# A 64-byte offset between TensorE's loaded and streamed operands in a one-core hybrid decoder trunk

## The chip, the cores and the metric

The kernel runs on one core of a Trainium2 chip. The metric is the device time of one execution in microseconds (us). TensorE multiplies, VectorE, ScalarE and GpSimd (POOL in the profile) do the elementwise work, and the queue of SyncE (SP) issues the DMAs. The other cores are idle.

## The reference

A trunk of two residual layers works on one sequence of 2048 tokens of width 1024, in float32. Each layer is `x = x + rms_norm(layer(rms_norm(x, g)), g2)`.

```python
# layer 0: one input projection, then two groups of heads
parts = jnp.split(h @ w_in, _offsets(EVEN_SPLIT_SIZES), axis=-1)
q, kc, vc, ks, vs, kw, vw, g_logit, z_a, u, v, z_b = parts
a = nsa_attention(q, kc, vc, ks, vs, kw, vw, g_logit, ...) * jax.nn.silu(z_a)
b = spatial_gating(jax.nn.gelu(u), jax.nn.gelu(v), ...) * jax.nn.silu(z_b)
return jnp.concatenate([a, b], axis=-1) @ w_out
# layer 1: a convolution module
a, gl, z = jnp.split(h @ w_in, 3, axis=-1)
y = a * jax.nn.sigmoid(gl)
y = depthwise_causal_conv(y, dw_w, 31 taps) + dw_b
y = jax.nn.silu(layer_norm(y, ln_g, ln_b))
return (y * jax.nn.silu(z)) @ w_out
```

`nsa_attention` has 8 heads of 64 in 2 groups, and adds three branches by gates: over 127 compressed blocks, over the 8 blocks of 64 tokens that score best for a query, and over a window of 512 tokens.

## The kernel before

Nearly every product is made of three matmuls. A float32 operand is split into a high part in the format float32r and a low part, the rest (`split`, L112 to L119), and `hi*hi + hi*lo + lo*hi` is summed in PSUM. A matmul names two operands: the first is loaded into the array as weights, 128 columns at a time, the second streams past it, 128 to 512 columns long. In the profile's rows the streamed one stands first (`A<-hhi,whi` streams `hhi` past `whi`). Each matmul has a weight load of its own, and the load for the next matmul runs while the present one streams.

- `project` (twice, for 1024 tokens each) makes the input projections. `dense_T` (L155 to L157) loads weights and streams 512 tokens of the normalised input; `dense_N` (L167 to L171) loads 128 tokens and streams 256 or 280 weight columns. `load_w` fetches and splits a block of weights. The spatial mix (L355) loads `sw`.
- `attention` walks over 64 units of a query tile, a head group and a pair of heads. `scores` (L570, L571) loads `q` and streams K, in pieces of 128 to 512 columns. The probabilities are transposed (L702: the probabilities are loaded, the identity of 128 columns streams), split, and streamed past V, 256 columns at a time (L724, L725). The front part of a unit (scores and softmax) is interleaved with the back part of the unit before. q is loaded by DMA four units ahead, V and K when a query tile first needs them.
- `out1` and `out2` (`out_project`, L836 to L838) load 128 tokens (`b4`, or the tiles `h2`, `h3`, `h6`, `h7`) and stream 512 columns of the output weights. A quarter of the first output weights is kept in the buffers of V's last two chunks.
- `layer1_in` makes layer 1's projections with `dense_T`, 24 blocks of 256 weight columns, each with four groups of 24 matmuls. Beside it VectorE and GpSimd run the convolution, by a written table of beats of 5.12 us: VectorE a tap at L1128, ScalarE and GpSimd another at L1094 and L1095.

The order of the instructions is set when the program is built, by a scheduler over the emitted work. `tile` takes every buffer from a pool. `LINE = 256`: tiles of under 1024 bytes a partition that aren't a multiple of 256 bytes go to a pool of their own, and two unused tiles at the edges (`LEFT`, `RIGHT`) bring all pools to multiples of 256 bytes. So in the built program the loaded and the streamed operand both start at a multiple of 256 bytes in all but three of 12388 matmuls (those three lie 128 off, both of them alike).

Of the kernel before, what the change touches and what calls it, by code (L numbers as in the profile page):

```python
# [11 lines left out]
F32R = mybir.dt.float32r  # L12
# [7 lines left out]
P = 128  # L20
S = 2048
D = 1024
KT = D // P
# [14 lines left out]
FILL = 8  # L38
EARLY = 20
LINE = 256  # L40
LEFT, RIGHT = 96, 224
LATE = 2
OUT1 = [5, 7, 6, 4, 1, 3, 2, 0, *range(8, NT)]
# [37 lines left out]
class Trunk:  # L81
# [18 lines left out]
        self.keep.append(p)  # L100
        return p

    def tile(self, pool, shape, dt, tag, bufs=None):

        kw = {} if bufs is None else {"bufs": bufs}
        title, space, usual = self.pools[id(pool)]
        size = (2 if dt == BF16 else 4) * math.prod(shape[1:])
        if space is None and size % LINE and size < 1024:
            pool, tag, kw = self.odd, f"{title}_{tag}", {"bufs": bufs or usual}
        return pool.tile(shape, dt, name=self.name(tag), tag=tag, **kw)  # L110
# [16 lines left out]
        g.memset(e, -0.5)  # L127
        g.tensor_tensor(out, x, e, ALU.pow)

    def load_w(self, pool, pieces, home=None, hi_eng=None):  # L130

        nc = self.nc
        n = sum(p.shape[1] for p in pieces)
        room = -(-n // 64) * 64
        raw = self.tile(pool, [P, KT, room], F32, "wraw", 1)[:, :, :n]
        o = 0
        for p in pieces:
            w = p.shape[1]
            nc.sync.dma_start(raw[:, :, o:o + w], p.rearrange("(k p) n -> p k n", p=P))
            o += w  # L140
        where, tags = (self.rp, home) if home else (pool, ("whi", "wlo"))
        hi, lo = (self.tile(where, [P, KT, room], F32R, t)[:, :, :n] for t in tags)
        self.split(hi, lo, raw, hi_eng or nc.scalar, nc.vector if home else nc.gpsimd)
        return hi, lo

# [109 lines left out]
    def setup_sgu(self, pool):  # L255
        nc, a = self.nc, self.a
        wn = self.tile(pool, [P, D], F32, "xin", 4).rearrange("p (g j) -> p g j", g=8)
        nc.sync.dma_start(wn, a["even_sgu_w"][0].rearrange("g i j -> i g j"))
        nc.gpsimd.affine_select(out=wn, in_=wn, pattern=[[0, 8], [-1, P]], compare_op=ALU.is_ge,
                                fill=0.0, base=0, channel_multiplier=1)  # L260
        sw = self.tile(pool, [P, 2, 8, P], F32R, "sw")
        self.sw_hi, self.sw_lo = sw[:, 0], sw[:, 1]
        for q in range(2):
            pt = self.tile(self.ps, [P, 512], F32, "T", 3)
            for g in range(4):
                nc.tensor.transpose(pt[:, P * g:P * g + P], wn[:, 4 * q + g], self.ident)
            v = lambda t: t[:, 4 * q:4 * q + 4].rearrange("p g i -> p (g i)")
            self.split(v(self.sw_hi), v(self.sw_lo), pt, nc.scalar, nc.vector)
        self.sb = self.tile(pool, [P, 8], F32, "sb")
        nc.sync.dma_start(self.sb, a["even_sgu_b"][0].rearrange("g i -> i g"))  # L270
        self.sg = self.tile(pool, [P, 2, 512], F32, "sg")
        nc.sync.dma_start(self.sg[:, 0], a["even_sgu_ln_g"][0:1, :].to_broadcast([P, 512]))
        nc.sync.dma_start(self.sg[:, 1], a["even_sgu_ln_b"][0:1, :].to_broadcast([P, 512]))


    def project(self, half):
        nc, a = self.nc, self.a
# [3 lines left out]
        col = lambda c0, n: W[:, c0:c0 + n]  # L281
# [11 lines left out]
            h0 = next(self.first)  # L293
        else:
            h0 = self.h0
        wv = [self.load_w(self.wp, [col(C_V, 256)], hi_eng=nc.vector if half == 0 else None)]
        x1 = self.load_rows(self.rp, rows(t0 + 512), ("r2", "r3"))
        for _ in self.first:
            pass
# [19 lines left out]
                nc.sync.dma_start(dst[1, f:f + P, s], lo.bitcast(F32))  # L319

        gvs = [self.tile(self.rp, [P, 4, 512], F32, f"r{c}") for c in range(2)]
        wv.append(self.load_w(self.wp, [col(C_V + 256, 256)], hi_eng=nc.gpsimd))
        for i, w in enumerate(wv):
            for t in range(8):
                o = self.tile(self.ps, [P, 512], F32, "A")
# [56 lines left out]
        for i in range(2):  # L382
            w = self.load_w(self.wp, [col(C_Q + 256 * i, 256)])
            for j in range(2):
                f = 256 * i + P * j
# [161 lines left out]
    def load_q(self, qt, g):  # L547

        nc, ap = self.nc, self.ap_
        q = self.tile(ap, [P, 2, 4, P], F32R, "q", 4)  # L550
        src = self.q_d[:, 256 * g:256 * g + 256, P * qt:P * qt + P].rearrange("y (h d) t -> y d h t", d=64)
        for y, x in itertools.product(range(2), range(2)):
            nc.sync.dma_start(q[64 * x:64 * x + 64, y].bitcast(F32), src[y])
        return q
# [188 lines left out]
    def fill(self):  # L743

        for _ in self.rest:
            pass
        self.psx.close()
        self.pst = self.pool(self.psx, "pst", 1, PSUM)
        self.rx.close()
        self.w1x = self.ctx.enter_context(ExitStack())  # L750
        self.w1p = self.pool(self.w1x, "w1", side="right")
        self.kv2 = self.pool(self.w1x, "kv2", side="right")
        for c in (2, 3):
            self.V[c] = self.tile(self.kv2, [P, 4, 4, P], F32R, f"V{c}")

    def attention(self):
        units = [(qt, g, p) for qt in ATTENTION for g in range(2) for p in range(2)]
# [142 lines left out]
    def out1(self, banks):  # L900

        nc, a, lp = self.nc, self.a, self.lp
        order = OUT1
        slots = ("wraw", "whiA", "wloA")
        raws = dict(enumerate(self.raws))

        def load(n):
            if n < NT:
                raws[n] = self.tile(lp, [P, 16, P], F32, slots[(n + 2) % 3])
                self.load_raw(raws[n], order[n])  # L910

        w = self.w1
        places = [None, None, None, [(self.kv2, "Ps", 2)] * 2]
        for store in self.stores:
            store()
        gpost = self.load_gpost(0)
        last = lambda: self.wout_pieces(a["even_w_out"][0], [(lp, f"h{i}") for i in range(4, 8)], places, (3,), w, nc.gpsimd)
        hs, xs = {}, []
        for n, i in enumerate(order):
            s = P * i  # L920
            load(n + 2)
            raw = raws.pop(n)
            if n > 1:
                nc.scalar.activation(raw[:, 12:16], raw[:, 12:16], AF.Silu)
                nc.gpsimd.tensor_tensor(raw[:, 4:8], raw[:, 4:8], raw[:, 0:4], ALU.add)
                nc.vector.tensor_tensor(raw[:, 4:8], raw[:, 4:8], raw[:, 12:16], ALU.mult)
            lhs = [self.tile(lp, [P, KT, P], F32R, "b4", 5) for _ in range(2)]
            self.split(*lhs, raw[:, 4:12], nc.scalar, nc.vector)
            done = n in (4, 8)
            if done:  # L930
                first, norm, xs = min(i for i, _ in xs), [x for _, x in sorted(xs, key=lambda e: e[0])], []
            out = self.out_project(lhs, w, gpost, a["x"][0, s:s + P, :], self.x1_d[s:s + P, :], banks=banks)
            if n == 0:
                next(out)
                held = out, i
                continue
            if n == 1:
                last()
            if n == 1:
                next(out)  # L940
                *_, x = held[0]
                xs.append((held[1], x))
            *_, x = out
            xs.append((i, x))
            if done:
                hs[first // 4] = self.normed(lp, norm, self.gpre[:, 1], self.chunk_tags(first // 4),
                                             lambda k: self.tile(banks[k % 2], [P, 512], F32, "T", 1))
        return [hs[0], hs[1]]


    def layer1_in(self, inner, half, hs):
# [5 lines left out]
        def load():  # L957
# [12 lines left out]
                nc.sync.dma_start(raw[:, :, o:o + w], p.rearrange("(k p) n -> p k n", p=P))  # L970
                o += w
            where, tag = ((pool, "A"), (inner, "B"))[i % 2]
            hi = self.tile(where, [P, KT, 256], F32R, "whi" + tag)
            lo = self.tile(where, [P, KT, 256], F32R, "wlo" + tag)
            self.split(hi, lo, raw, nc.scalar, nc.gpsimd)
            self.busy("p", 4.5)
            self.ws.append((hi, lo))
# [191 lines left out]
    def gated_norm(self, c, hand):  # L1169
# [77 lines left out]
            nc.gpsimd.tensor_tensor(y, y, z, ALU.mult)  # L1247
        self.busy("p", 4.5)
        yield
        hi, lo = (self.tile(pool, [P, KT, 256], F32R, f"h{2 + 4 * (c % 2) + i}") for i in range(2))  # L1250
        for q, y in enumerate(Y):
            s = slice(4 * q, 4 * q + 4)
            self.split(hi[:, s], lo[:, s], y, nc.scalar, nc.gpsimd)
# [90 lines left out]
    def run(self):  # L1344
# [1 line left out]
        mid = self.ctx.enter_context(ExitStack())  # L1346
        c = self.pool(mid, "mid")
        self.Kc = self.tile(c, [P, 2, P], F32R, "Kc")
        self.Vc = self.tile(c, [P, 2, P], F32R, "Vc")
        self.gates = self.tile(c, [P, NT, 24], F32, "gates")  # L1350
        self.rx = self.ctx.enter_context(ExitStack())
        self.rp = self.pool(self.rx, "right", side="right")
# [7 lines left out]
        with ExitStack() as ctx:  # L1360
            self.kvx = ctx
            kv = self.pool(ctx, "kv")
            self.V = {c: self.tile(kv, [P, 4, 4, P], F32R, f"V{c}") for c in (1, 0)}
            self.K = self.tile(kv, [P, 2, 2, S], F32R, "K")
            self.ps = self.pool(ctx, "psa", 3, PSUM)
            self.psx = ctx.enter_context(ExitStack())
            self.psf = self.pool(self.psx, "psf", 1, PSUM)
            self.pst = None
            self.probs = self.pool(ctx, "probs")
            self.ap_ = self.pool(ctx, "attn")  # L1370
            self.attention_consts(self.ap_)
            self.attention()
# [32 lines left out]
```

## Time and profile before

| | |
|---|---|
| median of 3 runs | 2283.37 us (2282.74 to 2284.02) |
| the profiled execution | 2281.41 us |
| its span on the core | 2279.7 us |
| granted clock of TensorE, mean | 0.993 |
| TensorE busy, matmuls | 2206.6 us (97%), 12414 instructions |
| weight loads busy | 1911.1 us (84%), 12414 |
| VectorE busy | 1548.0 us (68%) |
| ScalarE busy | 1258.4 us (55%) |
| GpSimd busy | 1403.2 us (62%) |

Busy times are unions of the spans of an engine's instructions. Spans of matmuls overlap, as one still drains when the next begins, so neither the mean of one nor the busy share tells how fast they follow each other; that is read from their starts in the timeline. PE is TensorE's matmuls, PEld its weight loads.

### The profile page before, as it was taken

The numbers are of one execution on the slowest core, as the hardware profiler recorded it, in microseconds if no ns is written. First come the engines' busy times: TensorE is split into PE (matmuls) and PEld (weight loads), VectorE is DVE, ScalarE is ACT, GpSimd is POOL, SyncE is SP. The second block draws the span as 40 slices with busy tenths as digits, with TensorE's granted clock in tenths as the row PEclk, the third lists the DMA queues.
The fourth block names the chain that finished last, engine by engine and source line by source line (L and its number), as shares of the span: only waits on it lengthen the run. The fifth ranks groups of instructions, "written<-read, shape, count | busy, mean of one in ns | idle before, by whom it ended". The sixth has DMA issues, their size and how long they took to land.

```text
span 2279.7 us, 34587 instructions
## 1 busy us (share of the span) xinstructions
PE 2206.6 (97%) x12414; PEld 1911.1 (84%) x12414; DVE 1548.0 (68%) x3272; ACT 1258.4 (55%) x2345; POOL 1403.2 (62%) x1351
## 2 busy tenths in 40 slices
PE   8999999999989999999999989999999989998998
PEld 7898889988878999898998978888888778886877
DVE  3441324365248998888889944427998899999772
ACT  5241132253257888878888863426555575556463
POOL 5232222243237778667779645558999579999683
PEclk9999999999999999999999999999999999999999
DMA  6252231442381111101113144651222432224641
GB/s 159 95 188 90 79 107 53 141 139 78 91 239 52 36 41 29 29 20 27 29 54 110 43 158 152 217 196 47 83 74 84 139 111 65 74 93 146 224 166 65
DMA packets 244860, 229.19 MB, mean 101 GB/s; under 512 B 33841, under 2 KB 206897, under 8 KB 244432
## 3 DMA queue, kind: packets, MB, share of 16 engines
q1 hardware_dynamic: 244688, 226.98, 31.4%
q8 instruction: 98, 1.61, 0.3%
q14 instruction: 74, 0.61, 0.1%
HBM read 157.73 MB, written 69.21 MB: 100 GB/s over the span
## 4 chain that ended last, share of the span: by engine, by line
PE 66%; DVE 12%; POOL 10%; issue 5%; ACT 4%; DMA 2%; SPq 1%; DVEq 0%; POOLq 0%; ACTq 0%
POOL cacc L1095 8%; PE A L155 7%; PE A L156 7%; PE A L157 7%; PE T L702 7%; PE O L725 4%; PE A L570 4%; PE O L724 4%; DVE acc L1128 4%; PE A L836 4%; PE A L837 4%; PE A L838 4%; PE A L571 4%; PE A L169 2%; PE A L171 2%
## 5 line engine op out<-in xcount | busy, mean ns | idle before, releaser
L1128 DVE SCALAR_TENSOR_TENSOR acc<-y,const_taps,acc 128x1024 f32<-128x1024 f32 x304 | 378.9, 1281 | 4.0
L1095 POOL TENSOR_TENSOR cacc<-cacc,prod 128x1024 f32<-128x1024 f32 x145 | 371.4, 2567 | 15.0 <-ACT prod L1094 7.7
L119 POOL TENSOR_TENSOR wlo<-wraw,whi 128x2048 fp32r<-128x2048 f32 (+1 forms) x26 | 120.7, 4642 | 315.1 <-ACT whi L116 279.9
L119 DVE TENSOR_TENSOR ptl<-T,pth 128x512 fp32r<-128x512 f32 (+1 forms) x414 | 263.7, 659 | 20.5 <-ACT pth L116 17.8
L116 ACT CAST pth<-T 128x512 fp32r<-128x512 f32 (+1 forms) x414 | 221.6, 579 | 52.5 <-PE T L702 42.1
L1094 ACT ACTIVATE prod<-y,const_taps 128x1024 f32<-128x1024 f32 x145 | 165.2, 1149 | 140.7 <-POOL cacc L1095 140.5
L155 PE MATMUL A<-hhi,whi 128*128 128x512 f32 x608 | 238.3, 392 | 0.0
L157 PE MATMUL A<-hhi,wlo 128*128 128x512 f32 x608 | 237.4, 391 | 0.0
L156 PE MATMUL A<-hlo,whi 128*128 128x512 f32 x608 | 237.4, 390 | 0.0
L679 POOL TENSOR_SCALAR Ps<-Ps,attn_ssm,gates 128x256 f32<-128x256 f32 (+15 forms) x128 | 162.0, 1266 | 112.7 <-DVE attn_ssm L676 78.5
L725 PE MATMUL O<-ptl,V 128*128 128x256 f32 x824 | 221.9, 295 | 1.6 <-DVE ptl L119 0.6
L724 PE MATMUL O<-pth,V 128*128 128x256 f32 x824 | 223.2, 293 | 0.0
L570 PE MATMUL A<-K,q 128*128 128x320 f32 (+4 forms) x544 | 206.8, 384 | 7.8 <-DVE attn_smx L574 4.5
L571 PE MATMUL A<-K,q 128*128 128x320 f32 (+4 forms) x544 | 183.5, 343 | 0.0
L674 ACT ACTIVATE Ps<-Ps,attn_nm 128x256 f32<-128x256 f32 (+15 forms) x128 | 155.8, 1217 | 31.9 <-DVE attn_nm L672 29.9
L574 DVE CUSTOM_DVE_ANT_1 Ps<-A,attn_bm 128x512 f32<-128x512 f32 (+3 forms) x264 | 154.9, 611 | 24.3 <-PE A L571 12.5
L702 PE MATMUL T<-ident,Ps 128*128 128x128 f32 x1088 | 164.2, 273 | 2.4 <-DVE ptl L119 1.6
L725 PEld LDWEIGHTS O<-ptl,V 128*128 128x128 f32 x824 | 155.9, 189 | 9.2 <-DVE ptl L119 4.7
L724 PEld LDWEIGHTS O<-pth,V 128*128 128x128 f32 x824 | 156.1, 189 | 2.5
L155 PE MATMUL A<-h,whiB 128*128 128x512 f32 x384 | 149.6, 390 | 1.3 <-ACT b L1019 1.3
L156 PE MATMUL A<-h,whiA 128*128 128x512 f32 x384 | 150.8, 393 | 0.0
L155 PE MATMUL A<-h,whiA 128*128 128x512 f32 x384 | 149.8, 392 | 0.7 <-DVE y L1001 0.7
(388 smaller groups left out, 6203.6 us busy)
## 6 DMA issues: line engine op xcount, KB each, us to landing
wraw<-in_even_w_in_dram SPq DMA_DIRECT2D x24, 1024.0 KB, 6.0
q<-q_d SPq DMA_DIRECT2D x128, 128.0 KB, 2.9
wraw<-in_odd_w_in_dram SPq DMA_DIRECT2D x32, 512.0 KB, 4.6
x<-x_d SPq DMA_DIRECT2D x21, 512.0 KB, 3.4
a_d<-osum SPq DMA_DIRECT2D x128, 64.0 KB, 2.1
x<-in_x_dram SPq DMA_DIRECT2D x16, 512.0 KB, 5.5
x_d<-x SPq DMA_DIRECT2D x16, 512.0 KB, 2.6
wraw<-in_odd_w_in_dram SPq DMA_DIRECT2D x8, 1024.0 KB, 4.9
```

Source lines behind the costliest of these rows:

```text
L116: self.nc.scalar.copy(hi, src)
L119: lo_eng.tensor_tensor(lo, src, hi.bitcast(F32), ALU.subtract)
L155: nc.tensor.matmul(o, whi[:, k, wk], hhi[:, k], start=(k == 0), stop=False)
L156: nc.tensor.matmul(o, whi[:, k, wk], hlo[:, k], start=False, stop=False)
L157: nc.tensor.matmul(o, wlo[:, k, wk], hhi[:, k], start=False, stop=(k == KT - 1))
L570: nc.tensor.matmul(out, q[:, 0, r, :], K[:, g, ks], start=True, stop=False)
L571: nc.tensor.matmul(out, q[:, 1, r, :], K[:, g, ks], start=False, stop=True)
L702: nc.tensor.transpose(pt[:, c:c + P], ps[r], self.ident)
L724: nc.tensor.matmul(O, v, hi[:, c], start=(i + j == 0), stop=False)
L725: nc.tensor.matmul(O, v, lo[:, c], start=False, stop=(i + j == len(items) - 1))
L1095: nc.gpsimd.tensor_tensor(c["sum"], c["sum"], t, ALU.add)
L1128: v.scalar_tensor_tensor(acc, win, w, old, ALU.mult, ALU.add)
```

## The change

`tile` gets a parameter `shift`. With it, the tile is allocated 64 elements (256 bytes) longer, and the slice that begins `shift` elements in is used; an element has 4 bytes, so 16 are 64 bytes and 48 are 192. The shift is given to the tiles that matmuls load: the split weights of `load_w` (by default 16), the spatial mix's `sw`, `q`, V, the left halves of the output projections (`b4`, `h2`, `h3`, `h6`, `h7`), layer 1's weights and `Vc`. The blocks `wv`, which stream in `dense_N`, get 48, so that the unshifted loaded halves of the input lie 64 bytes ahead of them.

```diff
+OFF = 16
...
-    def tile(self, pool, shape, dt, tag, bufs=None):
+    def tile(self, pool, shape, dt, tag, bufs=None, shift=0):
+        if shift:
+            n = math.prod(shape[1:])
+            t = self.tile(pool, [P, n + LINE // 4], dt, tag, bufs)[:, shift:shift + n]
+            a = "abc"[:len(shape) - 1]
+            return t.rearrange(f"p ({' '.join(a)}) -> p {' '.join(a)}", **dict(zip(a, shape[1:])))
...
-    def load_w(self, pool, pieces, home=None, hi_eng=None):
+    def load_w(self, pool, pieces, home=None, hi_eng=None, shift=16):
...
-        hi, lo = (self.tile(where, [P, KT, room], F32R, t)[:, :, :n] for t in tags)
+        hi, lo = (self.tile(where, [P, KT, room], F32R, t, shift=shift)[:, :, :n] for t in tags)
...
-        sw = self.tile(pool, [P, 2, 8, P], F32R, "sw")
+        sw = self.tile(pool, [P, 2, 8, P], F32R, "sw", shift=OFF)
...
-        wv = [self.load_w(self.wp, [col(C_V, 256)], hi_eng=nc.vector if half == 0 else None)]
+        wv = [self.load_w(self.wp, [col(C_V, 256)], shift=3 * OFF, hi_eng=nc.vector if half == 0 else None)]
...
-        wv.append(self.load_w(self.wp, [col(C_V + 256, 256)], hi_eng=nc.gpsimd))
+        wv.append(self.load_w(self.wp, [col(C_V + 256, 256)], shift=3 * OFF, hi_eng=nc.gpsimd))
...
-        q = self.tile(ap, [P, 2, 4, P], F32R, "q", 4)
+        q = self.tile(ap, [P, 2, 4, P], F32R, "q", 4, shift=OFF)
...
-            self.V[c] = self.tile(self.kv2, [P, 4, 4, P], F32R, f"V{c}")
+            self.V[c] = self.tile(self.kv2, [P, 4, 4, P], F32R, f"V{c}", shift=OFF)
...
-            lhs = [self.tile(lp, [P, KT, P], F32R, "b4", 5) for _ in range(2)]
+            lhs = [self.tile(lp, [P, KT, P], F32R, "b4", 5, shift=OFF) for _ in range(2)]
...
-            hi = self.tile(where, [P, KT, 256], F32R, "whi" + tag)
-            lo = self.tile(where, [P, KT, 256], F32R, "wlo" + tag)
+            hi = self.tile(where, [P, KT, 256], F32R, "whi" + tag, shift=OFF)
+            lo = self.tile(where, [P, KT, 256], F32R, "wlo" + tag, shift=OFF)
...
-        hi, lo = (self.tile(pool, [P, KT, 256], F32R, f"h{2 + 4 * (c % 2) + i}") for i in range(2))
+        hi, lo = (self.tile(pool, [P, KT, 256], F32R, f"h{2 + 4 * (c % 2) + i}", shift=OFF) for i in range(2))
...
-        self.Vc = self.tile(c, [P, 2, P], F32R, "Vc")
+        self.Vc = self.tile(c, [P, 2, P], F32R, "Vc", shift=OFF)
...
-            self.V = {c: self.tile(kv, [P, 4, 4, P], F32R, f"V{c}") for c in (1, 0)}
+            self.V = {c: self.tile(kv, [P, 4, 4, P], F32R, f"V{c}", shift=OFF) for c in (1, 0)}
```

On every engine the built program has the same instructions in the same order as before. Six of them differ in the semaphores that they wait for: four on GpSimd in the first output projection, one on SyncE there, and one on VectorE at the start of attention. The addresses in the built program stand like this, modulo 256 bytes:

| matmuls | loaded minus streamed, before | after | streamed at, after |
|---|---|---|---|
| 512 columns, 6032 | 0 | 64 | 0 |
| 512 columns on V's buffers, 192 | 0 | 0 | 64 |
| 384 and 320 columns, 464 | 0 | 64 | 0 |
| 280 columns, 384 | 0 | 192 | 64 |
| 256 columns, 1952 | 0 | 64 | 0 |
| 256 columns of `wv`, 768 | 0 | 64 | 192 |
| 128 columns of the scores, 336 | 0 | 64 | 0 |
| transposes, 2106 | 0 | 0 | 0 |
| others, 154 | 0 | 0 | 0 or 128 |

## Rows read from the trace of the kernel before

**Rows 1.** The page of the profiled execution, its first line.

```profile
span 2279.7 us, 34587 instructions
```

**Rows 2.** Busy time by stage, all engines: stretch, length, busy and (instructions) of each.

```profile
core 0: us, PE busy (x) PEld busy (x) DVE busy (x) ACT busy (x) POOL busy (x), PEclk, DMA share, GB/s
0.00:640.00 640.00, 623.61 (x3461) 545.53 (x3462) 240.79 (x360) 201.61 (x347) 181.74 (x139) 0.99 0.37 113
640.00:1330.00 690.00, 671.11 (x4929) 617.26 (x4927) 589.07 (x2274) 570.28 (x1342) 504.43 (x869) 1.00 0.20 56
1330.00:1540.00 210.00, 203.80 (x928) 167.92 (x928) 76.97 (x101) 82.44 (x160) 101.95 (x118) 0.99 0.58 193
1540.00:1740.00 200.00, 200.00 (x884) 165.68 (x883) 179.81 (x144) 114.18 (x118) 186.98 (x72) 1.00 0.23 77
1740.00:1880.00 140.00, 129.05 (x585) 104.60 (x584) 129.81 (x104) 81.13 (x100) 98.74 (x35) 0.99 0.34 109
1880.00:2060.00 180.00, 180.00 (x796) 149.10 (x795) 178.97 (x145) 101.00 (x104) 175.33 (x64) 1.00 0.22 76
2060.00:2280.00 220.00, 199.03 (x842) 161.05 (x840) 152.57 (x148) 107.78 (x181) 153.98 (x58) 0.97 0.44 153
```

**Rows 3.** Groups by line and form, TensorE: out<-streamed,loaded, form, count, busy us, mean ns.

```profile
L155 PE MATMUL A<-hhi,whi 128*128 128x512 f32 x608 | 238.3, 392 | 0.0
...
L724 PE MATMUL O<-pth,V 128*128 128x256 f32 x824 | 223.2, 293 | 0.0
...
L570 PE MATMUL A<-K,q 128*128 128x512 f32 x232 | 101.6, 438 | 5.6 <-DVE attn_smx L574 3.4 <-DVE attn_cmx L574 1.5 <-DVE attn_ssm L676 0.2
...
L167 PE MATMUL A<-whi,hhi 128*128 128x256 f32 x256 | 72.0, 286 | 2.1 <-DVE whi L118 2.1
L570 PE MATMUL A<-K,q 128*128 128x320 f32 x192 | 67.7, 356 | 1.1 <-DVE attn_smx L574 0.5
```

**Rows 4.** Timeline of TensorE in layer 1: start us, us; 442 matmuls, first and last.

```profile
1900.05 0.39 PE L156 MATMUL A<-h,whiA 128*128 128x512 f32 x1
...
2000.01 0.39 PE L156 MATMUL A<-h,whiA 128*128 128x512 f32 x1
```

**Rows 5.** Timeline of TensorE in the second half's projections, 256 columns, 11 matmuls.

```profile
349.77 0.28 PE L171 MATMUL A<-whi,hlo 128*128 128x256 f32 x1
...
350.97 0.28 PE L167 MATMUL A<-whi,hhi 128*128 128x256 f32 x1
```

**Rows 6.** Timeline of TensorE there, 280 columns: first and last of 11.

```profile
422.10 0.29 PE L167 MATMUL A<-whi,hhi 128*128 128x280 f32 x1
...
423.38 0.29 PE L169 MATMUL A<-wlo,hhi 128*128 128x280 f32 x1
```

**Rows 7.** Timeline of TensorE after four transposes, 512 columns.

```profile
232.62 0.60 PE L407 MATMUL T<-ident,r 128*128 128x128 f32 x4
...
233.30 0.39 PE L156 MATMUL A<-hlo,whi 128*128 128x512 f32 x1
...
234.00 0.39 PE L156 MATMUL A<-hlo,whi 128*128 128x512 f32 x1
234.22 0.39 PE L157 MATMUL A<-hhi,wlo 128*128 128x512 f32 x1
...
235.15 0.39 PE L155 MATMUL A<-hhi,whi 128*128 128x512 f32 x1
```

**Rows 8.** Timeline of TensorE in attention, K streaming: first and the sixth start after.

```profile
885.01 0.39 PE L571 MATMUL A<-K,q 128*128 128x512 f32 x1
...
886.16 0.28 PE L724 MATMUL O<-pth,Vc 128*128 128x256 f32 x1
```

**Rows 9.** Timeline of weight loads in attention: four for transposes, then the next.

```profile
884.24 0.46 PEld L702 LDWEIGHTS T<-ident,Ps 128*128 128x128 f32 x4
884.67 0.19 PEld L570 LDWEIGHTS A<-K,q 128*128 128x128 f32 x1
```

**Rows 10.** Waits of TensorE, longest first: us in total, times, longest us.

```profile
PE A L570 <- DMA q<-q_d: 3.0, 2, 2.5
```

## The prediction

> **What bounds the kernel now.** I read the page first, then the busy time by stage, then single starts on TensorE. The page gives a span of 2279.7 us [rows 1]; the profiled execution took 2281.41 us and the median of the three runs is 2283.37 us, 2.0 us more. The sum below is made against 2281.4, and 2 us are added at the end. The table by stage [rows 2] shows TensorE busy for 2206.6 of 2280 us at a granted clock of 0.97 to 1.00, so all of it stands at the upper level, 2.4 GHz. In the projections (0 to 640 us) it is busy 97% and VectorE 38%; in attention (640 to 1330) it is busy 97% and VectorE 85%; in the first output projection (to 1540) 97%. In layer 1 (1540 to 2060) two engines are nearly full at once: VectorE has 179.8 of 200 us, then 129.8 of 140, and at last 178.97 of 180. So a faster TensorE is worth its whole gain up to 1540 us, except where attention waits, and little in the last part of layer 1.
>
> A busy TensorE says nothing about its pace: the mean of a 512-column matmul is about 390 ns [rows 3], since each one overlaps the next. The pace is read from starts. In layer 1 a clean stretch has 441 steps from 1900.05 to 2000.01 us [rows 4]: 99.96/441 = 226.7 ns for 512 columns. In the second half's projections ten steps of 256 columns take 1.20 us [rows 5]: 120 ns. The difference, 106.7 ns for 256 columns, is 0.417 ns a column, so streaming alone is 213.3 and 106.7 ns: **13.3 ns of every matmul are not streaming**, whatever its width. 13.3 ns is the time of 32 columns. In bytes it is 128 of the streaming operand or 64 of the loaded one, which arrives at half the pace (a load takes 107.5 ns, below, for 128 columns). That excess is what this change can touch.
>
> Is it a fixed price of swapping in new weights? Three things in the trace say no. With 280 columns, where the streaming operand starts now on an odd and now on an even multiple of 256 bytes, ten steps take 1.28 us [rows 6], 128 ns, of which 11.3 are excess. After four transposes of 128 columns the same matmuls at the same alignment run for eight steps at (235.15 - 233.30)/8 = 231 ns [rows 7], and only later settle. And in attention, with K streaming, five steps of 512 columns take 1.15 us, 230 ns [rows 8]. So the excess goes from 11 to 18 ns with the addresses and with the moment at which load and stream begin. I read it as the load of the next operand and the running stream meeting in the same part of the memory; no row shows such a meeting by itself.
>
> **The change, part by part.** No engine gets another instruction or another order; six instructions wait for one semaphore more or less, since shifted tiles border on other old tiles. Each of those waits is for work that stands far ahead in the order, so I cost them at nothing.
>
> What moves is the address of the loaded operand. Before, loaded and streamed operand both lie at 0 modulo 256 bytes in all but three of 12388 matmuls. After, the loaded one lies 64 bytes ahead, except in 192 matmuls against V (both at 64), the 384 of 280 columns (64 behind), the transposes and some 150 small ones.
>
> *The price of one matmul* is not in the trace, as no row has a 64-byte offset. Bounds: all 13.3 ns of excess go (226.7 to 213.3), or the excess grows from 13.3 to 18 ns, the worst pace shown [rows 7]. Between them I take **one step of 16 columns, 6.67 ns**, a shift of 64 bytes in the stream, so 220 and 113.3 ns. I choose it because the settled paces are whole numbers of such steps (226.7 is 34, 120 is 18), because the change moves the load by one step, and because it lies between the ends.
>
> The Trainium skill has a rule against this (TensorE: Matmul & The Clock Gate, "Step-by-step: what each phase is for"): TensorE reads the streaming operand and the weights by two independent ports, so that loading the next weights takes nothing from the running matmul. By that rule the offset changes nothing and the sum is 2281; that one alignment gives 231 and 227 ns [rows 4, 7] doesn't fit a fixed price per swap well, but it doesn't show the ports either.
>
> *The sum.* Counts come from the groups by form [rows 3] times the number of groups alike, and for layer 1 and the output projections from the code's loops.
> - Projections: 3 x 608 matmuls of 512 columns, 3 x 256 of 256, and 96 of 256 in the spatial mix: 2688 x 6.67 ns = 17.9 us. TensorE is 97% busy and VectorE 38%: all of it counts.
> - Attention: 2 x 824 + 128 of 256 columns, 2 x 232 + 96 of 512, 2 x 192 of 320, 160 of 384 and 256: 2880 x 6.67 = 19.2 us. VectorE is 85% busy, transposes stay bound by their own loads (four in 0.43 us, 107.5 ns each [rows 9]), and what was hidden behind TensorE comes to light. I take two thirds: 12.8 us.
> - First output projection: half of 1536 less the 192 on V: 576 x 6.67 = 3.8 us, in full.
> - Layer 1: 24 weight blocks with 96 matmuls each, 2304, would give 15.4 us. To 1740 us VectorE has 20 us to spare, and 884 x 6.67 = 5.9 us count; of the next 624 (4.2 us) half, 2.1, since both engines idle there by turns; of the last 796 (5.3 us) only VectorE's spare 1.0 us. Together 9.0. What is late next there is VectorE's convolution.
> - Tail, the second output projection: 768 x 6.67 = 5.1 us; TensorE is busy 199 of 220 us, I take 3.6.
>
> 17.9 + 12.8 + 3.8 + 9.0 + 3.6 = 47.1 us. 2281.4 - 47.1 = 2234.3, and with the 2.0 us of the median **2236 us**, 2.1% faster.
>
> *What it costs.* q and V are now written by DMA to addresses 64 bytes off a multiple of 256. TensorE waits for q 3.0 us in two waits [rows 10]; the rest is loaded four units ahead and hidden. If those two waits doubled, it would cost 3 us; if nothing happens, 0, which is what I take. The Trainium skill (DMA: Bandwidth & Descriptors, "How a descriptor splits into AXI transactions") says that a descriptor which doesn't start at a multiple of 256 bytes is cut into more transactions: my estimate from that page is 18 beats instead of 16 for a piece of 512 bytes, an eighth more, under 0.5 us on these waits.
>
> VectorE, ScalarE and GpSimd write the shifted halves. No row shows them at such an address; if each of those writes got dearer by 1%, it would be hidden behind TensorE up to 1540 us, and the little in layer 1 lies inside the range.
>
> **The rivals.**
>
> *The whole excess goes.* For: after four transposes one step is as short as 0.22 us [rows 7], so the excess isn't a floor. Against: no settled stretch is below 226.7. Then 512 columns gain 13.3 ns and 256 columns 12, as a load alone takes 107.5 [rows 9]: projections 24.3 + 10.4 = 34.7, attention 2880 x 12.5 x 2/3 = 24.0, output 7.7, layer 1 11.8 + 4.2 + 1.0 = 17.0, tail 7.2; 90.6 us, 2191, or 2193 by the median. The Trainium skill (TensorE: Matmul & The Clock Gate, "Wait — 56ns, not 53.3ns?") has 215.7 ns for back-to-back matmuls of 512 columns; by that, my estimate is that 11 of the 13.3 ns would go, about 2208.
>
> *Only the narrow ones gain.* A load covers all of a 256-column stream but half of a 512-column one, which may make up the collision later. Then 864 x 6.67 = 5.8 us in the projections and 1856 x 6.67 x 2/3 = 8.3 in attention: 2267, or 2269.
>
> *Nothing happens.* The excess is the price of the swap; the same 13.3 ns at 256 and 512 columns speaks for it, [rows 6 to 8] against. 2281, or 2283. The port rule above would give this too.
>
> *The settled pace is lost (slower).* The clean 226.7 is a state in which load and stream have found a place beside each other, and all operands at 0 modulo 256 may be what lets them settle. With the load 64 bytes ahead, the stream, twice as quick, runs into it soon after the start, and the unsettled pace of 231.3 ns [rows 7] would hold everywhere, as it nearly does with K [rows 8]. Place: the 1824 + 96 + 576 + 2304 + 768 = 5568 matmuls of 512 columns outside attention's scores; 4.6 ns x 5568 = 25.6 us, in full, since TensorE becomes still more the bound: 2307, or 2309. It decides as soon as the mean pace grows by more than 0.8 ns (4.6 us / 5568). Should the pace go up a whole step, to 233.3 and 126.7 ns, all terms turn round without a cover: 17.9 + 19.2 + 3.8 + 15.4 + 5.1 = 61.4 us, 2345.
>
> That the change doesn't do what it says is excluded: the built addresses are as told.
>
> **How the numbers follow.** One step less: 0.36. All excess gone: 0.12. Narrow ones alone: 0.12. Nothing: 0.18. Slower: 0.22, most of it at the unsettled pace, 0.05 at a whole step. About 0.2%, 4.6 us, is what a measurement here can tell from no change. Faster: 0.36 + 0.12 + 0.12 = 0.60; within 0.2%: 0.18; slower: 0.22. The likeliest case has its own range, 2225 to 2250 (attention giving between all and a third of its 19.2 us, layer 1 between 5 and 15). The range goes down to the case in which nearly all the excess is gone, 2195, and up to the unsettled pace, 2309; the whole step, some of the unsettled cases with attention added, and the lowest end stay outside.
>
> **What would show it.** Starts of 512-column matmuls 220 ns apart in a clean stretch of layer 1, and 113 ns for 256 columns: the forecast. 213 to 216: the whole excess. 226.7 again: the price of the swap. Over 228 without settling: the slower rival. The 280-column stretch and the 192 matmuls on V serve as controls, as their offsets are 64 behind and 0: V's should keep 226.7. In layer 1 VectorE should be over 99% busy, with TensorE waiting for L1001 or for the pools. I am wrong if the paces fall and the span doesn't, or if q's wait grows by more than 3 us.

## The result and the profile after

The change made the kernel **slower by 0.5%**: 2293.27 us, the median of 6 runs (2291.34 to 2295.75), against 2282.34 for the kernel before in the same runs (2281.30 to 2284.02). The ratio is 1.0052, with a 95% interval of 1.0041 to 1.0062. The mean granted clock is 0.993 before and after. The forecast was 2236.

The page of the profiled execution after (2292.25 us) begins with this line, to be held against [rows 1]:

```profile
span 2290.5 us, 34587 instructions
```

Starts on TensorE after, first and last of three stretches (start us, us, engine, line, operation, out<-streamed,loaded): layer 1 with 512 columns, where [rows 4] stood before; the second half's 256 columns, [rows 5]; and its 280 columns, [rows 6].

```profile
1949.79 0.39 PE L161 MATMUL A<-h,whiB 128*128 128x512 f32 x1
...
1974.99 0.39 PE L161 MATMUL A<-h,whiB 128*128 128x512 f32 x1
...
347.80 0.28 PE L175 MATMUL A<-wlo,hhi 128*128 128x256 f32 x1
...
353.92 0.28 PE L175 MATMUL A<-wlo,hhi 128*128 128x256 f32 x1
...
426.71 0.29 PE L173 MATMUL A<-whi,hhi 128*128 128x280 f32 x1
...
432.92 0.29 PE L175 MATMUL A<-wlo,hhi 128*128 128x280 f32 x1
```

The first stretch has 108 steps: 25.20/108 = **233.3 ns for 512 columns, where 226.7 stood**. The second has 54: 6.12/54 = **113.3 ns for 256 columns, where 120 stood**. The third has 49: 126.7 ns, where 128 stood. So two widths moved by one whole 16-column step, in opposite directions. The control shows that the offset is at work, and not the shifted tiles as such. These are the first and the last of 12 matmuls on V's buffer, both operands at 64, among others at 233.3:

```profile
1391.93 0.39 PE L842 MATMUL A<-V,b 128*128 128x512 f32 x1
...
1394.44 0.39 PE L844 MATMUL A<-V,b 128*128 128x512 f32 x1
```

2.51/11 = 228 ns, so here the old pace nearly stays (over all matmuls on V's buffers the mean step is 228.8 ns, before 227.1).

Busy time by stage after, all engines (stretch, length, busy and instructions of each), to be held against [rows 2]:

```profile
0.00:640.00 640.00, 625.98 (x3446) 537.01 (x3446) 239.45 (x352) 199.56 (x340) 181.60 (x138) 1.00 0.36 111
640.00:1330.00 690.00, 672.50 (x4940) 617.55 (x4940) 588.41 (x2279) 572.33 (x1348) 503.60 (x869) 1.00 0.21 57
...
1540.00:1740.00 200.00, 200.00 (x859) 160.29 (x858) 175.77 (x141) 111.78 (x116) 179.58 (x68) 1.00 0.22 74
...
1880.00:2060.00 180.00, 180.00 (x768) 144.93 (x768) 178.96 (x144) 103.25 (x110) 174.25 (x63) 0.99 0.21 74
```

The busy shares don't move: TensorE had 200.00 of 200 us in 1540 to 1740 before, and has them now. The counts in brackets tell it: 859 matmuls instead of 884 in that stretch (a ratio of 1.029, as 233.3 to 226.7), and 768 instead of 796 in the last part of layer 1. Attention holds 4940 instead of 4929.

The order of the matmuls is the same in both traces, so the n-th of one can be set beside the n-th of the other. The start after, less the start before:

| at (us of before) | 649 | 732 | 1363 | 1582 | 2066 | 2097 | end |
|---|---|---|---|---|---|---|---|
| later by (us) | 7.4 | 3.3 | -1.2 | 4.0 | 14.2 | 6.4 | 10.9 |

The projections and layer 1 lose. Of the 8.6 us that come back between 649 and 1363 us, 3.0 lie in attention itself (3.4 late at 665 us, 0.4 at 1336); the rest comes back beside it, at places where TensorE waits for other engines. So do 7.8 us in the 31 us at the start of the tail.

### The profile page after: what moved, and what is told of

It reads as the page before. It is cut to its first block, busy times and chain, and to the rows that moved or that the text cites. A ratio compares the mean times of both kernels' runs of the same rounds, so it can differ in the third digit from the quotient of the medians.

```text
span 2290.5 us, 34587 instructions
## 1 busy us (share of the span) xinstructions
PE 2230.3 (97%) x12414; PEld 1902.2 (83%) x12414; DVE 1548.2 (68%) x3272; ACT 1258.6 (55%) x2345; POOL 1402.1 (61%) x1351
## 4 chain that ended last, share of the span: by engine, by line
PE 71%; DVE 13%; POOL 7%; issue 3%; ACT 2%; DMA 2%; SPq 1%; DVEq 0%; POOLq 0%; ACTq 0%
PE A L161 9%; PE A L162 9%; PE A L163 9%; PE T L708 7%; POOL cacc L1101 4%; DVE acc L1134 4%; PE O L731 4%; PE A L576 4%; PE O L730 4%; PE A L844 4%; PE A L843 4%; PE A L842 4%; PE A L577 4%; PE A L177 2%; PE A L175 2%
## 5 line engine op out<-in xcount | busy, mean ns | idle before, releaser
L580 DVE CUSTOM_DVE_ANT_1 Ps<-A,attn_bm 128x512 f32<-128x512 f32 (+3 forms) x264 | 154.9, 612 | 22.6 <-PE A L577 11.4
L162 PE MATMUL A<-h,whiA 128*128 128x512 f32 x384 | 153.3, 399 | 0.0
L161 PE MATMUL A<-h,whiA 128*128 128x512 f32 x384 | 152.3, 398 | 0.7 <-DVE y L1007 0.7
```

What stands on the lines that cost most here:

```text
L161: nc.tensor.matmul(o, whi[:, k, wk], hhi[:, k], start=(k == 0), stop=False)
L162: nc.tensor.matmul(o, whi[:, k, wk], hlo[:, k], start=False, stop=False)
```

## The experiments

The theory after the result (A in the expectations) was: the pace is set by the difference of the two addresses, and what a difference does depends on the width. Medians here stand against the kernel before, run on the same chip.

### The narrow part alone

```diff
-    def load_w(self, pool, pieces, home=None, hi_eng=None, shift=16):
+    def load_w(self, pool, pieces, home=None, hi_eng=None, shift=0):
...
-        w = self.load_w(self.wp, [col(C_VS, P), col(C_VW, P + 24)])
+        w = self.load_w(self.wp, [col(C_VS, P), col(C_VW, P + 24)], shift=3 * OFF)
...
-        q = self.tile(ap, [P, 2, 4, P], F32R, "q", 4, shift=OFF)
+        q = self.tile(ap, [P, 2, 4, P], F32R, "q", 4)
```

The tiles `b4`, `whi`, `wlo` and `h2` to `h7` lose their shift in the same way.

> Only the operands of 256- and 280-column matmuls keep an offset of 64 bytes (V, Vc, sw loaded 64 ahead of what streams; wv and the 280-column block streamed at 192 past loads at 0). Every 512-column matmul and the scores are back at offset 0, but for the 192 output-projection matmuls on V's buffers, which now lie at 192 (-64). Theory A (the pace depends on the offset together with the width: 64 is one 16-column step better for narrow ones and one step worse for 512): 512 columns settle at 226.7 ns again, wv at 113.3 to 114, 280 columns at 121 or 128, and the time is 2282.3 - 4.5 (wv) - up to 2.6 (280) - 3 (attention) = 2272 to 2275 us. Rival B (the loss of the change comes from something that shifted tiles bring beside TensorE's reading, as slower writes into them): the narrow part alone gives nothing or a loss, 2282 or more, though wv runs at 113.3.

2276.94 us against 2280.72, ratio 0.9982 (0.9973 to 0.9991): faster, by 3.8 us where 7 to 10 were expected, and rival B falls. 512 columns are back at 227 ns; the 280-column ones gained nothing (128.3 ns), and the 192 on V's buffers, at -64, took 230.4. Then there is a surprise. These are the first and the last starts of a piece of the first half's `wv` matmuls and of the second half's, in this kernel:

```profile
53.80 0.28 PE L175 MATMUL A<-wlo,hhi 128*128 128x256 f32 x1
...
59.91 0.28 PE L175 MATMUL A<-wlo,hhi 128*128 128x256 f32 x1
...
347.80 0.28 PE L175 MATMUL A<-wlo,hhi 128*128 128x256 f32 x1
...
353.93 0.28 PE L177 MATMUL A<-whi,hlo 128*128 128x256 f32 x1
```

54 steps of 113 ns, and 52 of 118, at the same offset. Each pace holds for its whole run of some 230 or 300 matmuls. In the changed kernel, which has the same addresses there, both runs settled at 113.3; the best version below has the two paces of this one. So **one offset can have two settled paces**. Which of them comes changes within one kernel: the four longer pieces of the second half, with transposes between them, have means of 118, 114.5, 114.5 and 118 ns.

### The wide part alone

```diff
-        sw = self.tile(pool, [P, 2, 8, P], F32R, "sw", shift=OFF)
+        sw = self.tile(pool, [P, 2, 8, P], F32R, "sw")
...
-        wv = [self.load_w(self.wp, [col(C_V, 256)], shift=3 * OFF, hi_eng=nc.vector if half == 0 else None)]
+        wv = [self.load_w(self.wp, [col(C_V, 256)], shift=0, hi_eng=nc.vector if half == 0 else None)]
```

V, Vc, the second `wv` and the 280-column block lose their shift as well.

> The other half alone: all loaded operands of 512-column matmuls and of the scores lie 64 ahead (V's buffers too, since V is back at 0), the narrow ones are back at offset 0. Theory A: 512 columns at 233.3 ns, 256 columns at 120, and the time is that of the change plus what the narrow ones gave back: 2293.3 + 8 to 10 = 2301 to 2303 us. Rival B' (the two parts disturb each other where they alternate, and the 512-column ones lose only beside shifted narrow ones): 512 columns near 226.7 in the long stretches of layer 1 and the time within 5 us of 2282.

2301.86 us against 2280.72, ratio 1.0092 (1.0078 to 1.0106). The 512-column ones run at 233.3 without shifted narrow ones beside them, so rival B' falls. The two parts, -3.8 and +21.1 us, make 17.3, while the change cost 10.9; the medians are sure to 2 or 3 us each. By the starts in the traces the parts are -5.4 and +20.1, 14.7 against 10.9. The 3.8 us between them are seen: V's buffers (offset 0 in the change, -64 and 64 in the two parts) make 1.6, the 280-column block 0.6, and the second `wv` run, at 113.3 in the change, 1.4.

### Every offset in one run

```diff
+SCAN_1 = [0, 4, 8, 12, 16, 20, 24, 28, 32, 36, 40, 44, 48, 52, 56, 60, 2, 6, 14, 18, 30, 34, 62, 48]
...
-            hi = self.tile(where, [P, KT, 256], F32R, "whi" + tag, shift=OFF)
+            hi = self.tile(where, [P, KT, 256], F32R, "whi" + tag, shift=SCAN_1[i])
```

Lists of the same kind give the shifts of `load_w`, `wv`, V, `b4` and `h2` to `h7`, in elements of 4 bytes.

> Every weight block, left half and V chunk gets an offset of its own, from 0 to 252 bytes in steps of 16 (a few of 8), so that one run shows the pace against the offset: layer 1's 24 blocks, 22 blocks of the input projections, 16 left halves of the first and 8 of the second output projection, all of 512 columns; four blocks of 256 columns, two of 280 and V's four chunks. Theory A (the relative offset decides): equal offsets give equal paces (within 1.5 ns) in all four places; 0 gives 226.7, 64 gives 233.3, and the others lie on steps of 6.67 ns, some perhaps below 226.7. Rival C (any offset but 0 costs 512 columns a step, whatever its size): 233.3 everywhere but at 0. Rival D (the place or the producer decides, not the offset): paces that differ between the places at one offset by more than 3 ns.

The time was 2289.92 us in its one run. In this trace three blocks of layer 1 begin and end like this (offsets 0, 64 and 120; 93 steps each, of 226.7, 233.4 and 226.7 ns):

```profile
1533.29 0.39 PE L169 MATMUL A<-h,whiA 128*128 128x512 f32 x1
...
1554.37 0.39 PE L169 MATMUL A<-h,whiA 128*128 128x512 f32 x1
...
1621.61 0.40 PE L169 MATMUL A<-h,whiA 128*128 128x512 f32 x1
...
1643.32 0.39 PE L169 MATMUL A<-h,whiA 128*128 128x512 f32 x1
...
1999.83 0.39 PE L169 MATMUL A<-h,whiA 128*128 128x512 f32 x1
...
2020.91 0.39 PE L169 MATMUL A<-h,whiA 128*128 128x512 f32 x1
```

The blocks of layer 1 read in this way (a star: steps with a wait left out), and 256 columns from the next experiment:

| offset, bytes | 0 | 8 | 16 | 32 | 48 | 56 | 64 | 80 | 96 | 112 | 120 | 128 | 144 | 176 | 192 | 208 | 224 | 240 | 248 |
|---|---|---|---|---|---|---|---|---|---|---|---|---|---|---|---|---|---|---|---|
| 512 columns, ns | 226.7 | 230.7 | 226.7 | 233.3 | 233.3 | 233.3 | 233.3 | 231.9 | 234.2 | 233.3 | 226.7 | 233.4 | 233.3 | 230.3* | 228.9* | 232.6* | 233.2* | 228.5 | 233.3 |
| 256 columns, ns | 119.9 | 115.6 | 118.3 | 118.3 | 117.8 | 117.8 | 113.3 | 118.8 | 117.3 | 120.0 | - | 118.6 | 118.3 | 118.1* | 116.4* | 116.8* | 116.7* | 120.0 | 117.6 |

Not in the table: 512 columns gave 231.1 ns at 24 bytes, 233.4 at 72 and 233.3 at 136 and 160; 256 columns gave 118.3 at 4, 68 and 72, 119.5 at 60 and 120.0 at 160. Within a block the loaded operand moves by 1024 bytes from one k to the next and the streamed one by 2048, so their difference also changes by multiples of 256 there, and the pace stays.

At 0, 32, 64, 96, 160 and 224 the input projections, layer 1 and the output projections agree within 1.6 ns, so rival D falls at 0 and 64, the offsets of the kernel. By its own measure of 3 ns it stands at two others: in the short runs of the first output projection 144 gave 228.7 ns (233.3 elsewhere) and 192 gave 233.3 (229.0 elsewhere). Rival C falls at 16 and 120. So does the part of theory A that put all paces on steps of 6.67 ns: 8, 24, 80, 192 and 240 bytes hold means between 226.7 and 233.3. **No offset gives 512 columns less than the 226.7 ns that 0 gives**; for 256 columns, 0 is among the worst and 64 the best.

### Two halves of 256, and the streamed side shifted

```diff
-                nc.tensor.matmul(o, whi[:, k, wk], hhi[:, k], start=(k == 0), stop=False)
+                    nc.tensor.matmul(o[:, s], whi[:, k, wk], hhi[:, k, s], start=(k == 0), stop=False)
...
-        parts = [self.tile(home or pool, [P, n, 512], F32R, t, 1) for t in tags]
+        parts = [self.tile(home or pool, [P, n, 512], F32R, t, 1, shift=16 if self.nw < 0 else None) for t in tags]
```

In layer 1 `s` goes over two halves of 256 columns; `nw` is negative in layer 0.

> Three things at once. (1) In layer 1 each 512-column matmul is made of two of 256 columns with the same operands (so twice as many weight loads there, and 3 to 4 per cent more time in all), and the 24 blocks have 24 offsets. Theory A (width and offset together decide): at 64 a 256-column step is 113.3 to 114 ns and at 0 it is 120, in the same place where 512 columns had 233.3 and 226.7; two halves at 64 then take 227, as one 512-column matmul at 0 does. Rival D (the place decides): layer 1 shows no gain at 64, 118 to 120 everywhere. (2) In the input projections the streamed halves themselves lie 64 off, with loaded blocks at shifts of 0 to 252 bytes. Theory A in its narrow form (only the difference of the two addresses counts): 512 columns at 226.7 where both lie at 64, 233.3 where the loaded one is 64 ahead at 128, and wv, unshifted, runs at 114 with its load at 64. Rival E (it is the loaded operand's own address that counts): 226.7 where the loaded block lies at 0, that is at a difference of -64. (3) The left halves of the output projections get offsets of 4 to 252 bytes in odd multiples of 4, to see whether a pace below 226.7 ns exists between the offsets measured so far: by theory A none is known, and a pace of 220 at any of them would be new.

The time was 2310.19 us in its one run, 1.2% over the kernel before (3 to 4 per cent were expected). Layer 1's blocks at offsets 0 and 64 in its trace:

```profile
1533.27 0.28 PE L173 MATMUL A<-h,wloA 128*128 128x256 f32 x1
...
1550.91 0.28 PE L173 MATMUL A<-h,wloA 128*128 128x256 f32 x1
...
1624.32 0.28 PE L172 MATMUL A<-h,whiA 128*128 128x256 f32 x1
...
1640.87 0.28 PE L171 MATMUL A<-h,whiA 128*128 128x256 f32 x1
```

17.64/147 = 120.0 ns and 16.55/146 = 113.4 ns: with the same operands in the same place, 256 columns gain where 512 lose. Two halves at 64 take 226.8 ns together, what one matmul of 512 takes at 0. In the projections, with the streamed side at 64, the differences 0, 64, 80, 96, 120, 144 and 192 gave 226.9, 233.3, 231.9, 234.3, 227.0, 233.3 and 229.0 ns: the paces of the run before within 0.3. A loaded block at address 0 (difference 192) ran at 229.0, not 226.7, so rival E falls, and `wv`, unshifted, ran at 114.2 with its load at 64. The difference decides, with exceptions. One pair breaks the row: 16 gave 233.3 here and 226.7 there, again two paces at one offset. At odd multiples of 4 bytes the output projections showed 230 to 234 ns, and nothing below 226.7.

### Shorter loads

```diff
...
+                for n, (x, y) in enumerate(((whi, hhi), (whi, hlo), (wlo, hhi))):
+                    m = P if (k, n) in ((0, 0), (KT - 1, 2)) else SCAN_M[self.nw - 1]
+                    nc.tensor.matmul(o[:m], x[:, k, c0:c0 + m], y[:, k], start=(k == n == 0), stop=(k == KT - 1 and n == 2))
```

> In layer 1 most matmuls load only the first 128, 96, 64, 32 or 16 of the 128 weight columns, block by block (all but the first and the last matmul of each accumulation), so the rest of the output rows lacks these terms; the 512 streamed columns and their number stay. The offsets of the blocks are 0, 16, 32, 64, 80, 96, 120, 128, 160 and 192. Theory G (the excess over 213.3 ns is the load of the next operand meeting the running stream, so it grows with the length of the load): at offset 0 the pace falls with the loaded columns, from 226.7 at 128 towards 220 at 64 and 213 to 217 at 16, and the dependence on the offset dwindles with it (64 columns: at most half of the 6.7 ns between offsets 0 and 64). Rival H (a fixed price of swapping the operands, to which the offset only adds): 226.7 at offset 0 for every number of loaded columns, and 226.7 or more at all other offsets.

The time was 2285.78 us in its one run. The groups of weight loads in layer 1 of this kernel, by form (out<-streamed,loaded, form, count, busy us, mean ns of one):

```profile
L164 PEld LDWEIGHTS A<-h,whiA 128*64 128x64 f32 x300 | 40.4, 135 | 27.7
...
L164 PEld LDWEIGHTS A<-h,wloA 128*128 128x128 f32 x104 | 19.5, 188 | 6.8
...
L164 PEld LDWEIGHTS A<-h,whiA 128*16 128x16 f32 x60 | 5.7, 95 | 7.8
```

And starts of matmuls that loaded 16 columns each, at offset 64, first and last of 19:

```profile
2036.73 0.62 PE L164 MATMUL A<-h,whiA 128*16 128x512 f32 x2
...
2040.90 0.40 PE L164 MATMUL A<-h,whiA 128*16 128x512 f32 x1
```

The record of a load of 16 columns is half as long as that of 128, and the step is 4.17/18 = 231.7 ns. At offset 0 the means are 227.2, 230.2, 229.6, 231.3 and 230.8 ns for 128, 96, 64, 32 and 16 loaded columns; at 64 they are 233.3, 229.0, 232.6, 231.5 and 231.7. **The first half of theory G falls**: at offset 0 the excess over 213.3 ns does not shrink with the load, it grows. Its second half comes true: from offset 0 to 64 the pace changes by 6.1 ns with 128 loaded columns, and by -1.2, 3.0, 0.2 and 0.9 with 96, 64, 32 and 16. So the length of the load has a part in what the offset does, though not as theory G had it. Rival H falls as well, since the pace at offset 0 rises when the loads get shorter. In all blocks of this run the excess is 13 to 21 ns a matmul, without growing with the loaded columns.

### Other widths

```diff
+            n = SCAN_N[self.nw - 1]
...
+                nc.tensor.matmul(o[:, :n], whi[:, k, wk], hhi[:, k, :n], start=(k == 0), stop=False)
```

> In layer 1 the blocks stream 504, 496, 480, 448, 416, 384, 352, 320, 288, 272, 256 or 240 columns instead of 512, each width once at offset 0 and once at 64 (the remaining columns get one matmul instead of 24, so their sums lack terms). The excess is the settled step less 0.417 ns a column. Theory I (the sign of the offset's effect follows the width: a narrow stream gains, a wide one loses): the step at 64 is under that at 0 up to some width between 256 and 512, and above it beyond. Rival J (no trend: each pair of width and offset falls on a pace of its own, as a rhythm of load and stream that happens to fit): the signs change from one width to the next, and 256 and 512 happen to be of different sign. At 256 columns 113 to 120 by both, at 504 or 496 columns 13 or 20 ns of excess by theory I.

The time was 2289.18 us in its one run. The excess in ns (mean settled step less 0.417 ns a column):

| columns | 240 | 256 | 272 | 288 | 320 | 384 | 416 | 448 | 480 | 496 | 504 |
|---|---|---|---|---|---|---|---|---|---|---|---|
| at 0 | 12.0 | 13.3 | 12.0 | 11.7 | 13.3 | 13.3 | 14.3 | 16.0 | 16.8 | 15.1 | 16.7 |
| at 64 | 12.2 | 7.1 | 10.0 | 13.6 | 13.3 | 14.2 | 13.3 | 15.6 | 16.0 | 13.3 | 18.9 |

Steps with a wait are left out, and so are 352 columns, since TensorE ran at the lower clock level in part of them (granted clock 0.85 from 1740 to 1880 us). Of the differences over 1.5 ns, 64 is the better offset at 256, 272 and 496 columns and the worse one at 288 and 504: theory I falls, and rival J fits. Without 256 no width of this row moves by more than 2.2 ns; 512 moves by 6.6 in the runs above. At offset 0, 504 columns take 226.7 ns, as 512 do.

### Layer 1 alone

Only `whi` and `wlo` of `layer1_in` keep their shift; all else is as before.

> Only layer 1's weight blocks are shifted by 64 bytes (2304 matmuls of 512 columns at 233.3 instead of 226.7 ns), all else is as before. Priced as TensorE time in full (rival F) that is 2304 x 6.5 = 15 us: 2296 us. Theory A with the cover of the other engines: the loss collects through layer 1, and where the tail begins TensorE waits 8 us less for the splits of GpSimd, ScalarE and VectorE than before; 5 to 8 us remain: 2287 to 2289 us.

2285.30 us against 2280.09, ratio 1.0019 (1.0010 to 1.0028): 5.2 us, and rival F falls. By starts, matmuls are 11.4 us later than before at 2066 us, 3.3 at 2097, and 4.2 at the end. What TensorE waited for in 2060 to 2110 us in the kernel before (us in total, times, longest):

```profile
PE A L836 <- ACT late_ors L859: 3.3, 1, 3.3
PE A L837 <- DVE h L119: 2.7, 1, 2.7
PE A L837 <- DVE wloB L119: 1.7, 1, 1.7
PE A L836 <- ACT whiB L116: 1.1, 1, 1.1
PE A L838 <- POOL h L119: 0.2, 1, 0.2
```

In the kernel with layer 1 shifted that stretch has no wait at all. TensorE came 11 us later, and the work of the other engines that it had waited 9.0 us for was ready.

### The best version

```diff
-        w = self.load_w(self.wp, [col(C_VS, P), col(C_VW, P + 24)], shift=3 * OFF)
+        w = self.load_w(self.wp, [col(C_VS, P), col(C_VW, P + 24)], shift=OFF)
...
-        self.w1[1, 0] = [self.V[c].rearrange("p k y d -> p k (y d)") for c in (2, 3)]
+        self.w1[1, 0] = [t[:, :2048].rearrange("p (k n) -> p k n", k=4) for t in self.w1[1, 0]]
```

The diff is against the narrow part alone; its second change takes V's last two buffers from their unshifted start (the lines of `fill` that keep the buffers are left out).

> The narrow part alone, mended at two places: the 280-column block streams at 64 past loads at 0 (difference -64, as in the change, 126.7 ns instead of 128.3), and the output weights that take V's last two buffers start at their unshifted beginning, so that those 192 matmuls of 512 columns are back at a difference of 0 (227 ns instead of 230.4). Theory A: 384 x 1.6 ns + 192 x 3.4 ns = 1.3 us under the narrow run, that is 5 us under the kernel before (ratio 0.9977 to 0.998). The rival, that these paces are hidden behind other work there, gives the narrow run's 0.9982.

2274.43 us against 2280.09, ratio **0.9977 (0.9968 to 0.9986)**: faster than the kernel before by the interval, and so than the changed one. By starts the end lies 7.1 us before that of the kernel before, against 5.4 for the narrow run; the medians don't tell these two apart, as the rival's 0.9982 lies inside the interval.

## Why the prediction was wrong

**The bound was read rightly.** TensorE sets the pace up to 1540 us, but for the waits told below, and its pace is read from starts: the busy shares stayed while everything took longer.

**"The price of one matmul" failed.** The text took one step of 16 columns less for every width, and gave as reasons that settled paces are whole steps, that the change moves the load by one step, and that the value lies between the ends. The first holds for the two paces after (113.3 is 17 steps, 233.3 is 35), but not in general: 512 columns held 230.7 ns at 8 bytes, and 256 columns 115.6. The second does not carry either: a step of 64 bytes moved 512 columns up. For 256 columns the price was right to 0.1 ns in the long runs of `wv`, and too high in attention (below). For 512, with most of the time, it had the wrong sign: 6.6 ns up where 6.67 down was taken. Nothing in the trace before gave a sign: all rows there lie at one offset. The excess was also held to be 13.3 ns "whatever its width", which two widths had shown; at offset 0 the other widths have 11.7 to 16.8. Two rivals hold half of what happened: narrow ones gain, as in the second, and for the wide ones the last one's whole step up came true, at 233.3. The measured time lies between the stated 2195 and 2309 only because that range took in a slower case, the unsettled pace; that pace is not what came.

**The reading under it was not borne out.** "The load of the next operand and the running stream meeting in the same part of the memory" would let one expect less excess with a shorter load, and at offset 0 there was more. That the load has a part in it is shown all the same, since with 16 loaded columns the offset hardly matters (231.7 ns at 64, 230.8 at 0). Where the two meet, if they do, no run shows. The Trainium skill (TensorE: Matmul & The Clock Gate, "Step-by-step: what each phase is for") says that loading the next weights takes no read bandwidth from the running matmul. By that alone the offset would have no effect, which 226.7 ns against 233.3 contradicts. The shorter loads agree so far: 95 instead of 188 ns of load, and a step that is no shorter. The Trainium skill (TensorE: Matmul & The Clock Gate, "Wait — 56ns, not 53.3ns?") has 215.7 ns for back-to-back matmuls of 512 columns; no settled stretch here reached it, and 226.7 is the least.

**The terms.** With one step up instead of down, the projections' 1824 wide ones would cost 1824 x 6.6 = 12.0 us. In the wide part alone matmuls are 10.0 us late at 632 us, and in the narrow part alone 4.2 early. With both they are 6.4 late, where the forecast had them 17.9 early. At the start of attention 4.2 us come back, from 7.6 at 650 us to 3.4 at 665, and that is no faster matmul. TensorE waits there for ScalarE's copy `zst`, which empties the buffer of its next matmuls (before and after; us in total, times, longest):

```profile
PE F L155 <- ACT zst L437: 3.6, 1, 3.6
PE F L161 <- ACT zst L443: 0.8, 1, 0.8
```

Behind the long wait the matmuls of the kernel before came 427 ns apart at a granted clock of 0.50 (660.7 to 663.5 us), which "all of it stands at the upper level" had passed over; behind the short one the clock was 1.00. The wide part, whose narrow matmuls are as before, gets 5.0 back in the same place. Attention itself, from 665 to 1336 us, gives 3.0 (forecast 12.8). Its 256-column matmuls go from 118.6 to 116.0 ns in the mean of all steps without a wait, 2.6 less instead of 6.7, and its 512-column ones stay, 231.8 and 232.1. They come a few at a time between transposes; that they don't settle for this reason is a reading and was not tried. Another 1.6 come back to 1363 us, where the first output projection begins with waits for splits.

Between 1363 and 2066 us the first output projection and layer 1 cost 15.4 (forecast -3.8 and -9.0). The tail returns 3.3: 7.8 at its start, less 4.5 for its own wide ones. The whole-step rival, priced "without a cover", had every term as a loss, 61.4 us. What is missing in it is narrow ones that gain and waits that a later TensorE no longer meets: some 4 us at the start of attention and 8 at that of the tail.

**What cost nothing.** The waits for q were put at nothing, with 3 us as the other end. TensorE's waits for it after (us in total, times, longest):

```profile
PE A L576 <- DMA q<-q_d: 2.2, 3, 1.5
PE A L577 <- DMA q<-q_d: 2.0, 3, 0.8
```

4.2 us, where L570 of [rows 10] and L571 (1.3 us) had 4.3. The median landing of q is 3.0 us instead of 2.9. The control on V nearly held, at 228.8 ns for the 226.7 that was stated. Shifted writes show nowhere either. VectorE's busy 178.96 us in 1880 to 2060, as before to 0.01 [rows 2], doesn't tell, as it is full there either way; its busy time in all does, with the same instructions: 1548.0 us before, and after

```profile
PE 2230.3 (97%) x12414; PEld 1902.2 (83%) x12414; DVE 1548.2 (68%) x3272; ACT 1258.6 (55%) x2345; POOL 1402.1 (61%) x1351
```

with ScalarE and GpSimd at 1258.4 and 1403.2 before.

**Open.** Why a pair of width and offset settles where it does was not found: the runs show paces that repeat from place to place, some of them whole steps, and sometimes two at one offset. What decides between the two was not tried.

## What to carry to other kernels

A settled pace at one alignment, whole number of steps or not, says nothing of which way another alignment goes. Change one operand's offset block by block in one run, read the pace from starts, and choose per width: here 64 bytes for 256 columns, 0 for 512. Count a settled pace only where runs are long: in attention 256 columns gained 2.6 ns, in the long runs 6.7. A loss of TensorE ahead of a place where it waits for other engines is partly given back there, just as a gain is partly lost: the narrow part alone was 4.2 us early at 632 us and 2.4 at 732.

## What was not expected of the hardware

- The step between matmuls of 512 columns moves from 226.7 to 234.2 ns with the difference of two addresses modulo 256, in jumps: 0, 16 and 120 bytes gave 226.7, and 112 and 136 beside 120 gave 233.3.
- For 256 columns the 113.3 ns at 64 bytes stands alone: 60 gave 119.5 and 68 gave 118.3.
- Fewer loaded columns make a matmul no quicker: 16 of 128 load in 95 instead of 188 ns, and the step goes from 227.2 to 230.8 ns at offset 0.
- The same operands at the same addresses ran at 113 or at 118 ns a step for hundreds of matmuls.
